# First stage of a two-layer diffusion step: loads and modulation products in another order, modulation ends and first norm scheduled ahead

## Chip, cores and metric

One NeuronCore of a Trainium2 chip runs the whole program. The metric is the device time of one launch in microseconds (us). Everything is float32; products with a split operand run as three float32r products (high x high, high x low, low x high).

## What is computed

Two transformer-like layers over 384 tokens (128 prompt tokens, 256 latent tokens). What matters here is the opening of each layer and the one thing that runs beside it:

```python
mod = (silu(cond) @ w_mod + b_mod)          # (1, 6*1024): sh1, sc1, g1, sh2, sc2, g2
h = rms_norm(x, norm1) * (1 + sc1) + sh1    # input of every mixer
proj = h @ w_in                             # 1024 x 6048; its Hyena columns come first in the kernel
kf = hyena_filters(L, w1, b1, w2, b2, w3, freq)   # an MLP with sines, window, L1 norm, DFT
```

`kf` depends on no token, so it can be computed beside anything that comes before the long convolution. `h` needs x, two of the six parts of `mod` (shift, part 0, and scale, part 1), and so 2 x 4 MB of `w_mod`.

## The kernel before, in words

Tokens stand in columns: `xa` is 128 x 8 x 384, eight chunks of 128 channels. One program text is written as Python generators ("lines"), each `yield` a step, and `weave` (line 1334) takes steps from side lines at a rate per step of a main line. The text gives each instruction its place (priority); a planner then fixes at compile time the order on every engine, from priorities and from its own idea of durations. At run time each engine works through its own list in order. `tc.high_priority(offset=n)` counts the instructions in it as if they stood n places earlier in the text; `urgent(line, n)` (line 1318) does so for every step of a line. Nothing else decides the order.

The parts of the first stage:

- `filters(0, ...)` (line 440) is the Hyena filter. Its first step loads the MLP's inputs; then come two sine layers (`reduce_sin`, line 423, with a chain of eight VectorE/ScalarE instructions each, and one product each, lines 460 and 464); then `half_inputs(0)` loads `w3` and the window for one half of the channels and `kdft`, the DFT table; then `half_inputs(1)` the other half. After that come four jobs: `prep` (line 483), three `taps` (line 498, products of line 503), three `sizes` (line 517) and `spectra` (line 531, products of lines 538, 546 and 558).
- `mod_load` (line 326) loads one 1 MB slice of `w_mod`. `mod_vec(l, v)` (line 332) makes part v: for each of four slices k, four products of line 338 into one PSUM bank; then a ScalarE copy, four transposes (line 302) into the same bank, two small VectorE sums, and for part 1 the scale `avs` (line 241 as `stt`). The bank line `md` has one bank (bank 7), so part 1 starts after part 0's sums are out.
- `squares` (line 314) squares and adds the eight chunks of x. `norm_h` (line 373) makes the reciprocal root on a diagonal, spreads it over 128 partitions by a product (line 388), and then, chunk by chunk: multiply (VectorE), scale and shift on ScalarE (line 396, one for each token stream), and the split into high and low parts (lines 403 and 231, then a subtraction).
- `hyena_start` (line 615) issues two loads of `w_in` (`load_w`, line 247), each split by ScalarE (line 231) and VectorE (line 235) in two halves. The main line `hyena_in` (line 634) then makes six outputs of 8 x 3 products each (lines 269 to 271). Its first product needs the first chunk of h and the first half of the first weight load.

The eight early `w_mod` slices lie in buffers that later have another use: two in the raw ring of the weight loads, four in the slab of the split weights, two in the slab of h. Only SP issues loads in this stage. The order of the text was: MLP inputs, `vecs`, `cT`; the two sine layers; `half_inputs(0)` and `kdft`; `w_mod` 0/0 and 0/1 (part/slice), identity; `half_inputs(1)`; `w_mod` 0/2 and 0/3, both halves of x, `w_mod` 1/0 to 1/3, silu. Then a `weave` of the two `mod_vec` with three filter steps and 1.2 squares for each of their steps (12 steps of `mod_vec`, so 36 of the filter's 49 steps stand in it). Then `hyena_start`, the whole norm, the rope tables and the second `vecs`, and the loop over layers, whose first `weave` takes two filter steps for each step of `hyena_in`.

Of the kernel before, what the change touches and what calls it, by code (L numbers as in the profile page):

```python
# [41 lines left out]
SLABS = (1408, *[3072] * 9)  # L42
N_EXTRA = 3584
R_RE = 0.25
R_F0 = 3
U_CH, U_MLA = 20, 20
U_AV = 2000
FILL = (3, 2, 3)
# [137 lines left out]
def kernel(  # L186
# [127 lines left out]
    def squares():  # L314
        for k in range(KD):
            add_sq(k, xa[:, k], k == 0)
            yield
# [8 lines left out]
    def mod_load(l, v, k, buf):  # L326
        raw = buf.ap(2, 1024)
        src = w_mod[l, k * 256:(k + 1) * 256, v * 1024:(v + 1) * 1024]
        sp.dma_start(out=raw, in_=src.rearrange("(k p) n -> p k n", p=128))
        return raw  # L330

    def mod_vec(l, v, ready=(), bufs=()):

        gv = ps_of("md", 512)
        for k in range(KD // 2):
            raw = ready[k] if k < len(ready) else mod_load(l, v, k, raw_ring.get())
            for j in range(4):
                pe.matmul(  # L338
                    gv[32 * j:32 * j + 32], cT[:, 2 * k + j // 2], raw[:, j // 2, (j % 2) * 512:(j % 2) * 512 + 512],
                    start=k == 0, stop=k == KD // 2 - 1, tile_position=(0, 32 * j),  # L340
                )
            if bufs:
                bufs.pop(0).free()
            yield
        ms = mod_s
        copy_a(ms.ap(), gv)
        yield
        pm = ps_of("md", 4, 128)
        for q in range(4):
            transpose(pm[:, q], ms.ap()[:, q * 128:(q + 1) * 128])  # L350
# [89 lines left out]
    def filters(l, R, spec, first=False):  # L440
# [8 lines left out]
        def half_inputs(hf):  # L449
            w3 = FA.alloc(4, 256)  # L450
            sp.dma_start(out=w3.ap(1024), in_=p_w3[l, hf])
            wb = FA.alloc(5, 256)
            sp.dma_start(out=wb.ap(1280), in_=p_win[l, hf])
            return wb, w3
# [14 lines left out]
        h.free()  # L469
        yield  # L470
        inputs = [half_inputs(0), None]
        kd = [FA.alloc(10, 128)] if first else [R.alloc(10, 128) for _ in range(2)]
        kt = [b.ap() for b in kd]
        kv = t_kdft.rearrange("p (a b) -> p a b", b=128)
        if first:
            sp.dma_start(out=kt[0], in_=kv)
        yield
        if first:
            inputs[1] = half_inputs(1)
            yield  # L480
        jobs = {}
# [847 lines left out]
    def finish(*lines):  # L1329
        for g in lines:  # L1330
            for _ in g:
                pass
# [11 lines left out]
    def chain(*lines):  # L1344
        for g in lines:
            yield from g
# [21 lines left out]
    next(fl)  # L1368
    sp.dma_start(out=vecs[0], in_=p_vec[0])
    sp.dma_start(out=cT, in_=p_c)  # L1370
    next(fl)
    next(fl)
    next(fl)
    ready = [mod_load(0, 0, k, early[k]) for k in range(2)]
    sp.dma_start(out=ident, in_=t_ident)
    next(fl)
    for k in (2, 3):
        ready.append(mod_load(0, 0, k, early[k]))
    for k in (0, 4):
        sp.dma_start(out=xa[:, k:k + 4], in_=p_x[:, k:k + 4])  # L1380
    for k in range(4):
        ready.append(mod_load(0, 1, k, early[4 + k]))
    act.activation(out=cT[:, :, 0:2], in_=cT[:, :, 0:2], func=AF.Silu)
    weave(chain(mod_vec(0, 0, ready[:4]), mod_vec(0, 1, ready[4:])), (fl, R_F0), (squares(), 1.2))
    for b in early_parts:
        b.free()
    parts = split_slab.whole(F32R).cut(1024)
# [2 lines left out]
    h_parts += [b.ap(KD, T) for b in h_slab.whole(F32R).cut(KD * T)]  # L1390
    hT = h_parts
    y, main = hyena_start(0, spec)
    finish(norm_h(0, 0))
    for i in range(2):
        rt = t_rope[i * 128:(i + 1) * 128]
        sp.dma_start(out=rope_a[:, i], in_=rt[:, 0:128].rearrange("p (a b) -> p a b", a=2))
        sp.dma_start(out=rope_b[:, i], in_=rt[:, 128:192].rearrange("p (a b) -> p a b", a=2))
    sp.dma_start(out=vecs[1], in_=p_vec[1])
    for l in range(NL):
        md = chain(*[mod_vec(l, v) for v in (2, 3, 4, 5)]) if l == 0 else chain(nxt.pop().steps, mod_vec(l, 4))  # L1400
        banks(**PS_HY0)
        weave(main, (md, R_MD), (fl, R_FL))
        finish(fl)
        hyena_open(y)
        oC = y.oT
        banks(**PS_HY1)
# [196 lines left out]
```

## Time and profile before

| | us |
|---|---|
| runs: median of 3 (lowest, highest) | 1504.46 (1504.19, 1507.05) |
| profiled execution, its own time | 1503.74 |
| span of the profiled execution | 1501.6 |
| TensorE busy, of the span | 1455.7 |
| VectorE busy | 1006.0 |
| ScalarE busy | 751.3 |
| mean rate of the loads over the span | 142 GB/s |

The time of an execution is its span and 2.1 us around it. In the rows below PE is TensorE (PEld its weight loads), DVE VectorE, ACT ScalarE, POOL GpSimd, SP the engine that issues loads; "L338" is line 338. A timeline row has the start, the time the (merged) instructions took, the engine, the line, the operation with what it writes and reads, the count, and in brackets how long the engine sat idle before it and what ended that. `base`, `split`, `h` and `s` are memory slabs: a load of `w_in` lands in `base` and is split into `split`, and `banks` is PSUM. A float32 product is recorded as two.

### The profile page before, as it was taken

What the parts mean: (1) busy time and instruction counts of PE and PEld (TensorE: products, weight loads), DVE (VectorE), ACT (ScalarE), POOL (GpSimd) and SP (SyncE); (2) the same over time, 40 slices, a digit from 0 to 9 for tenths busy, and PEclk for the clock granted to TensorE, in tenths of its full rate; (3) what the DMA queues carried; (4) which work ended last, traced back from release to release, by engine and by line L of the source; (5) the groups of instructions that cost most, each with busy time, mean ns of one, the idle gap of its engine ahead of it and who ended that gap; (6) DMA issues with size and microseconds to landing.
All of it is one profiled execution on the core that took longest, in us unless ns stands there. A gap on an engine that the chain in (4) does not pass through costs nothing.

```text
span 1501.6 us, 22071 instructions
## 1 busy us (share of the span) xinstructions
PE 1455.7 (97%) x8542; PEld 1337.6 (89%) x8542; DVE 1006.0 (67%) x1920; ACT 751.3 (50%) x1376; POOL 106.4 (7%) x133
## 2 busy tenths in 40 slices
PE   5799999999999999999998999999999999999997
PEld 2588789989889899999996988999888989999997
DVE  6768569547457896686766767884655767567674
ACT  4545356555544663463545444855555454344343
POOL 1223210000000001010000212100000000000000
PEclk9899999999999999999999999999999999999999
DMA  9444454433466543343276446332333523433431
GB/s 362 151 153 138 136 166 138 119 113 113 141 224 228 187 137 103 122 130 113 85 246 204 139 135 182 91 106 83 97 118 111 195 100 117 135 105 122 153 119 50
DMA packets 177496, 212.84 MB, mean 142 GB/s; under 512 B 24176, under 2 KB 160112, under 8 KB 177392
## 3 DMA queue, kind: packets, MB, share of 16 engines
q1 hardware_dynamic: 176528, 206.99, 42.7%
q0 software_dynamic: 864, 4.46, 1.0%
q8 instruction: 67, 1.10, 0.3%
q14 instruction: 37, 0.30, 0.1%
HBM read 209.29 MB, written 2.13 MB: 141 GB/s over the span
## 4 chain that ended last, share of the span: by engine, by line
PE 90%; DVE 4%; ACT 3%; DMA 2%; issue 1%; SPq 0%; DVEq 0%; ACTq 0%
PE banks L269 26%; PE banks L270 26%; PE banks L271 25%; PE banks L302 3%; PE banks L338 3%; PE banks L922 3%; DVE s L238 2%; PE banks L954 2%; DMA base<-in_w_in_dram 1%; DVE split L235 1%; PE banks L558 1%; ACT split L231 1%; ACT s L231 1%; PE banks L503 0%; DVE s L241 0%
## 5 line engine op out<-in xcount | busy, mean ns | idle before, releaser
L231 ACT ACTIVATE split<-base 128x1024 fp32r<-128x1024 f32 (+2 forms) x272 | 280.9, 1041 | 366.9 <-PE banks L270 258.5
L235 DVE TENSOR_TENSOR split<-base,split 128x1024 fp32r<-128x1024 f32 (+2 forms) x272 | 331.8, 1225 | 181.5 <-ACT split L231 179.4
L269 PE MATMUL banks<-h,split 128*128 128x384 f32 x1280 | 433.3, 342 | 5.0 <-DVE h L403 3.6
L270 PE MATMUL banks<-h,split 128*128 128x384 f32 x1280 | 435.2, 340 | 0.1
L271 PE MATMUL banks<-h,split 128*128 128x384 f32 x1280 | 434.2, 340 | 0.0
L269 PEld LDWEIGHTS banks<-h,split 128*128 128x128 f32 x1280 | 241.4, 189 | 20.7 <-issue 9.9
L270 PEld LDWEIGHTS banks<-h,split 128*128 128x128 f32 x1280 | 242.0, 189 | 4.5 <-issue 1.3
L271 PEld LDWEIGHTS banks<-h,split 128*128 128x128 f32 x1280 | 241.7, 189 | 2.2 <-issue 0.5
L270 PE MATMUL banks<-s,split 128*128 128x384 f32 x672 | 225.8, 337 | 0.0
L271 PE MATMUL banks<-s,split 128*128 128x384 f32 x672 | 225.4, 338 | 0.0
L269 PE MATMUL banks<-s,split 128*128 128x384 f32 x672 | 223.2, 339 | 1.0 <-ACT s L231 0.8
L241 DVE SCALAR_TENSOR_TENSOR s<-banks,base,s 128x127 f32<-128x127 f32 (+1 forms) x448 | 172.8, 411 | 11.9 <-ACT s L417 7.9
L231 ACT ACTIVATE s<-banks 128x384 f32<-128x384 f32 (+11 forms) x212 | 94.3, 471 | 99.1 <-PE banks L271 37.9
L231 ACT ACTIVATE s<-s 128x384 fp32r<-128x384 f32 (+3 forms) x142 | 79.0, 562 | 106.0 <-DVE s L238 57.2
L269 PEld LDWEIGHTS banks<-s,split 128*128 128x128 f32 x672 | 125.6, 188 | 4.4 <-ACT s L231 1.4
L271 PEld LDWEIGHTS banks<-s,split 128*128 128x128 f32 x672 | 126.1, 188 | 2.0 <-DVE base L241 0.8
L270 PEld LDWEIGHTS banks<-s,split 128*128 128x128 f32 x672 | 126.1, 188 | 1.4 <-issue 0.2
L238 DVE TENSOR_TENSOR s<-banks,s 128x512 f32<-128x512 f32 (+3 forms) x132 | 81.6, 645 | 37.7 <-PE banks L271 16.7
L241 DVE SCALAR_TENSOR_TENSOR base<-banks,base 128x128 f32<-128x128 f32 (+1 forms) x128 | 46.9, 413 | 73.8 <-PE banks L271 73.8
L238 DVE TENSOR_TENSOR s<-s 128x256 f32<-128x256 f32 (+4 forms) x122 | 69.0, 576 | 23.0 <-ACT s L1225 8.4
L417 ACT ACTIVATE s<-banks,base 128x384 f32<-128x384 f32 x112 | 73.2, 655 | 13.2 <-PE banks L271 13.2
L302 PE MATMUL banks<-base,s 128*128 128x128 f32 x442 | 75.2, 274 | 2.8 <-DVE s L241 1.7
(146 smaller groups left out, 1730.4 us busy)
## 6 DMA issues: line engine op xcount, KB each, us to landing
base<-in_w_in_dram SPq DMA_DIRECT2D x40, 1024.0 KB, 5.4
base<-in_ffn_up_dram SPq DMA_DIRECT2D x40, 1024.0 KB, 5.1
base<-in_w_mod_dram SPq DMA_DIRECT2D x28, 1024.0 KB, 5.3
s<-in_w_mod_dram SPq DMA_DIRECT2D x14, 1024.0 KB, 7.5
base<-in_ffn_down_dram SPq DMA_DIRECT2D x16, 896.0 KB, 4.6
base<-in_w_branch_dram SPq DMA_DIRECT2D x24, 512.0 KB, 3.5
base<-in_w_out_dram SPq DMA_DIRECT2D x8, 1024.0 KB, 5.1
base<-in_ffn_down_dram SPq DMA_DIRECT2D x8, 1024.0 KB, 5.0
```

The lines of the kernel that those rows point to most:

```text
L231: act.activation(out=out, in_=in_, func=AF.Copy, scale=scale)
L235: dve.tensor_tensor(out=lo, in0=src, in1=f(hi), op=ALU.subtract)
L238: dve.tensor_tensor(out=out, in0=a, in1=b, op=op)
L241: dve.scalar_tensor_tensor(out=out, in0=a, scalar=s, in1=b, op0=op0, op1=op1)
L269: pe.matmul(out, l[0], r[0], start=start, stop=False)
L270: pe.matmul(out, l[0], r[1], start=False, stop=False)
L271: pe.matmul(out, l[1], r[0], start=False, stop=stop)
L302: pe.transpose(out, in_, ident[:n, :n])
L338: pe.matmul(gv[32 * j:32 * j + 32], cT[:, 2 * k + j // 2], raw[:, j // 2, (j % 2) * 512:(j % 2) * 512 + 512], start=k == 0, stop=k == KD / ...
L417: act.activation(out=dst, in_=src, func=AF.Identity, scale=vec(l, w1), bias=vec(l, bias))
L922: pe.matmul(out, q_of(h)[:, i * 128:(i + 1) * 128], k, start=m == 0, stop=m == len(ks) - 1)
L954: last = pe.matmul(p[b:b + 64, u], v, pT, start=start, stop=stop, tile_position=(0, b)).ins
```

## The change

The filter's steps 4 and 5 are cut differently: the step that loads `half_inputs(0)` now ends there, and `kdft` and `half_inputs(1)` are steps 5 and 6. The loads stand in the text as: MLP inputs, `vecs`, `cT`, silu, `w_mod` 0/0 and 0/1; then after the first sine layer the products of these two slices; after the second the identity, `half_inputs(0)`, `w_mod` 0/2, `kdft`, `w_mod` 0/3, x, `w_mod` 1/0 and 1/1, `half_inputs(1)`, `w_mod` 1/2 and 1/3. The end of a modulation part is a function of its own, `mod_end`, without the step between copy and transposes, and for parts 0 and 1 of layer 0 it is placed 300 instructions ahead; the first norm is placed 150 ahead. `mod_vec` has five steps in place of six, two of them are taken before the `weave`, and the filter's rate in it is 3.5: eight main steps, 28 filter steps. The rope tables and the second `vecs` are loaded after the `weave` of `hyena_in`.

```diff
--- before.py
+++ after.py
@@ -42,7 +42,8 @@
 SLABS = (1408, *[3072] * 9)
 N_EXTRA = 3584
 R_RE = 0.25
-R_F0 = 3
+R_F0 = 3.5
+U_MD, U_N0 = 300, 150
 U_CH, U_MLA = 20, 20
 U_AV = 2000
 FILL = (3, 2, 3)
@@ -342,9 +343,13 @@
             if bufs:
                 bufs.pop(0).free()
             yield
+        with ExitStack() as order:
+            order.enter_context(tc.high_priority(offset=U_MD if (l, v) in ((0, 0), (0, 1)) else 0))
+            yield from mod_end(l, v, gv)
+
+    def mod_end(l, v, gv):
         ms = mod_s
         copy_a(ms.ap(), gv)
-        yield
         pm = ps_of("md", 4, 128)
         for q in range(4):
             transpose(pm[:, q], ms.ap()[:, q * 128:(q + 1) * 128])
@@ -469,13 +474,13 @@
         h.free()
         yield
         inputs = [half_inputs(0), None]
+        yield
         kd = [FA.alloc(10, 128)] if first else [R.alloc(10, 128) for _ in range(2)]
         kt = [b.ap() for b in kd]
         kv = t_kdft.rearrange("p (a b) -> p a b", b=128)
         if first:
             sp.dma_start(out=kt[0], in_=kv)
-        yield
-        if first:
+            yield
             inputs[1] = half_inputs(1)
             yield
         jobs = {}
@@ -1368,20 +1373,24 @@
     next(fl)
     sp.dma_start(out=vecs[0], in_=p_vec[0])
     sp.dma_start(out=cT, in_=p_c)
+    act.activation(out=cT[:, :, 0:2], in_=cT[:, :, 0:2], func=AF.Silu)
+    ready = [[mod_load(0, 0, k, early[k]) for k in range(2)], []]
+    md = chain(*[mod_vec(0, v, ready[v]) for v in range(2)])
     next(fl)
+    next(md)
+    next(md)
     next(fl)
-    next(fl)
-    ready = [mod_load(0, 0, k, early[k]) for k in range(2)]
     sp.dma_start(out=ident, in_=t_ident)
     next(fl)
-    for k in (2, 3):
-        ready.append(mod_load(0, 0, k, early[k]))
+    ready[0].append(mod_load(0, 0, 2, early[2]))
+    next(fl)
+    ready[0].append(mod_load(0, 0, 3, early[3]))
     for k in (0, 4):
         sp.dma_start(out=xa[:, k:k + 4], in_=p_x[:, k:k + 4])
-    for k in range(4):
-        ready.append(mod_load(0, 1, k, early[4 + k]))
-    act.activation(out=cT[:, :, 0:2], in_=cT[:, :, 0:2], func=AF.Silu)
-    weave(chain(mod_vec(0, 0, ready[:4]), mod_vec(0, 1, ready[4:])), (fl, R_F0), (squares(), 1.2))
+    ready[1] += [mod_load(0, 1, k, early[4 + k]) for k in (0, 1)]
+    next(fl)
+    ready[1] += [mod_load(0, 1, k, early[4 + k]) for k in (2, 3)]
+    weave(md, (fl, R_F0), (squares(), 1.2))
     for b in early_parts:
         b.free()
     parts = split_slab.whole(F32R).cut(1024)
@@ -1390,17 +1399,18 @@
     h_parts += [b.ap(KD, T) for b in h_slab.whole(F32R).cut(KD * T)]
     hT = h_parts
     y, main = hyena_start(0, spec)
-    finish(norm_h(0, 0))
-    for i in range(2):
-        rt = t_rope[i * 128:(i + 1) * 128]
-        sp.dma_start(out=rope_a[:, i], in_=rt[:, 0:128].rearrange("p (a b) -> p a b", a=2))
-        sp.dma_start(out=rope_b[:, i], in_=rt[:, 128:192].rearrange("p (a b) -> p a b", a=2))
-    sp.dma_start(out=vecs[1], in_=p_vec[1])
+    finish(urgent(norm_h(0, 0), U_N0))
     for l in range(NL):
         md = chain(*[mod_vec(l, v) for v in (2, 3, 4, 5)]) if l == 0 else chain(nxt.pop().steps, mod_vec(l, 4))
         banks(**PS_HY0)
         weave(main, (md, R_MD), (fl, R_FL))
         finish(fl)
+        if l == 0:
+            for i in range(2):
+                rt = t_rope[i * 128:(i + 1) * 128]
+                sp.dma_start(out=rope_a[:, i], in_=rt[:, 0:128].rearrange("p (a b) -> p a b", a=2))
+                sp.dma_start(out=rope_b[:, i], in_=rt[:, 128:192].rearrange("p (a b) -> p a b", a=2))
+            sp.dma_start(out=vecs[1], in_=p_vec[1])
         hyena_open(y)
         oC = y.oT
         banks(**PS_HY1)
```

## Rows read from the trace of the kernel before

**Rows 1.** Page, first part, whole span: engine, busy us, share, instructions.
```profile
PE 1455.7 (97%) x8542; PEld 1337.6 (89%) x8542; DVE 1006.0 (67%) x1920; ACT 751.3 (50%) x1376; POOL 106.4 (7%) x133
```

**Rows 2.** Windows, first stage: us, busy per engine, PEclk, DMA share, GB/s.
```profile
25.00:30.00 5.00, 4.91 (x32) 3.80 (x24) 4.17 (x8) 4.31 (x10) 2.42 (x3) 1.00 1.01 411
...
35.00:40.00 5.00, 4.09 (x19) 1.36 (x17) 3.47 (x8) 3.09 (x5) 1.06 (x2) 1.00 1.06 364
...
50.00:55.00 5.00, 3.91 (x20) 2.45 (x18) 5.00 (x9) 2.12 (x3) 1.82 (x1) 1.00 0.51 145
55.00:60.00 5.00, 0.00 (x0) 0.00 (x0) 5.00 (x9) 0.63 (x1) 1.58 (x1) 0.57 0.25 73
60.00:65.00 5.00, 4.80 (x12) 4.08 (x13) 4.11 (x13) 4.99 (x12) 1.44 (x2) 0.50 0.57 201
65.00:70.00 5.00, 5.00 (x26) 3.43 (x26) 3.50 (x9) 5.00 (x13) 0.00 (x0) 0.90 0.24 52
```

**Rows 3.** Timeline, TensorE: start us, us, engine, line, operation, count [idle before].
```profile
47.31 1.06 PE L338 MATMUL banks<-h,base 128*32 128x512 f32 x8
...
49.80 0.66 PE L302 MATMUL banks<-base 128*128 128x128 f32 x4 [0.37 <-ACT base L231]
...
60.20 1.22 PE L558 MATMUL banks<-s 128*128 128x256 f32 x2 [5.93 <-DVE s L540]
...
63.42 1.52 PE L269 MATMUL banks<-h,split 128*128 128x384 f32 x3
```

**Rows 4.** Timeline, VectorE, from the transposed sums to the last normed chunk.
```profile
53.01 0.17 DVE L238 TENSOR_TENSOR base<-banks,base 128x16 f32<-128x16 f32 x1
...
54.02 2.06 DVE L235 TENSOR_TENSOR split<-base,split 128x1024 fp32r<-128x1024 f32 x1
...
59.26 0.16 DVE L238 TENSOR_TENSOR base<-base,banks 128x16 f32<-128x16 f32 x1
...
60.06 0.17 DVE L241 SCALAR_TENSOR_TENSOR base<-base 128x16 f32<-128x16 f32 x1
...
72.33 1.02 DVE L235 TENSOR_TENSOR h<-s,h 128x384 fp32r<-128x384 f32 x2
```

**Rows 5.** Load issues: last w_mod slices, SP timeline, then us to landing.
```profile
L329 SPq DMA_DIRECT2D h<-in_w_mod_dram x2: 1440/1925/2410, 17.9 to 19.5; - x2
...
33.53 18.16 SPq L249 DMA_DIRECT2D base<-in_w_in_dram  x3
...
h<-in_w_mod_dram SPq DMA_DIRECT2D x1, 1024.0 KB, 20.7
...
base<-in_w_in_dram SPq DMA_DIRECT2D x1, 1024.0 KB, 10.8
```

**Rows 6.** Groups of TensorE products, 46 to 63.4 us: count, busy us, mean ns.
```profile
L558 PE MATMUL banks<-s,s 128*128 128x256 f32 x11 | 3.8, 472 | 0.0
L558 PE MATMUL banks<-s 128*128 128x256 f32 x4 | 2.3, 674 | 5.9 <-DVE s L540 5.9
L503 PE MATMUL banks<-s 128*128 128x512 f32 x6 | 2.3, 479 | 0.4 <-DVE s L238 0.4
L546 PE MATMUL banks<-s,base 128*128 128x512 f32 x2 | 1.1, 644 | 0.0
...
L538 PE MATMUL banks<-base,s 128*128 128x1 f32 x8 | 1.0, 249 | 0.0
```

**Rows 7.** Timeline, start of the filter work: VectorE, then TensorE.
```profile
7.60 0.43 DVE L238 TENSOR_TENSOR s<-s 128x256 f32<-128x256 f32 x1 [1.74 <-DMA s<-in_p_w_dram]
...
8.21 1.08 DVE L238 TENSOR_TENSOR s<-s 128x256 f32<-128x256 f32 x3
...
9.60 0.69 DVE L238 TENSOR_TENSOR s<-s,s 64x512 fp32r<-64x512 f32 x1
...
13.75 1.65 PE L464 MATMUL banks<-s 64*128 64x384 f32 x2 [8.60 <-ACT s L436]
...
16.46 0.15 PEld L338 LDWEIGHTS banks<-base 128*32 128x32 f32 x4 [0.93 <-DMA base<-in_w_mod_dram]
```

## Prediction

> **What bounds the kernel now.** The page comes first: TensorE is busy 97% of the span [rows 1], so a change pays only where TensorE is idle or slow. The windows tell where that is. From 65 us on TensorE is full; before, 55 to 60 us holds no product at all, and 60 to 65 us runs at a granted clock of 0.50, the 1.2 GHz level, after 0.57 in the stretch before [rows 2]. VectorE is the full engine there: 5.00 of 5.00 us in both windows from 50 to 60 us [rows 2].
>
> The timeline of TensorE shows what comes out late. The last products of modulation part 1 start at 47.31 us, their transposes at 49.80, and the first product of the main line at 63.42; between lies the idle stretch of 5.93 us that ends at 60.20 [rows 3]. The timeline of VectorE says why. The transposes end at 50.46 (49.80 + 0.66), but the two sums that read them run at 53.01 and 59.26 and the scale at 60.06 [rows 3, 4]: three instructions of 0.16 to 0.17 us, spread over 7 us in VectorE's list, among splits of weights (two in 2.06 us at 54.02) and filter work. No operand is missing; the order put them there. Norm and main line wait for the scale, which is out at 60.23.
>
> The last `w_mod` slice does not explain it: issued at 19.5 us, it lands 20.7 us later, at 40.2, but its products start 7.1 us after that [rows 3, 5]. The transfers are the floor under all this, as the load engines are fully busy (1.01) at 411 GB/s [rows 2].
>
> **The change, part by part.**
>
> *Modulation end ahead.* New start of the last products: about 40.4. The bytes before that slice are the same, and the order inside them does not move the last one. From there to the scale: product to end of the transposes took 3.15 us (47.31 to 50.46) [rows 3], in which ScalarE was also splitting a weight, so this is rather an upper price; the three small instructions add 0.50 [rows 4] if VectorE takes them at once, and about 0.2 for their handovers by my estimate. Scale out at 44.2 at the latest, 43.4 without ScalarE's delay; I take 43.8. That is 16.4 us earlier than 60.23.
>
> *Norm ahead.* The step from scale to first main product was 3.2 us (60.23 to 63.42) [rows 3, 4]; I keep it: first product at 47.0. The part of the norm that needs no modulation (root, spread, four of the chunk products, as the eight buffers of `temps` hold four pairs) lies before that, beside the loads. The weights must not be later: the first `w_in` load was issued at 33.53 and landed 10.8 us after, at 44.3 [rows 5]. Its split costs one ScalarE and one VectorE instruction, about 1.03 us each by VectorE's pair in 2.06 [rows 4], so it is ready at 46.4. It is the next thing in line, half a microsecond behind.
>
> *Work owed.* An earlier start is not all gain: the filter products that filled 46 to 63.4 us must still run, now beside a full TensorE. They are L558 3.8 and 2.3, L503 2.3, L546 1.1 and L538 1.0 us [rows 6]. The 2.3 ran at half clock (674 ns each against 472 in a mixed stretch [rows 6]), so I count it and the 3.8 as 3.6 together: 8.0 us owed. Bounds: 6.8, if some of it still fits before 47, and 10.5, all as recorded. The modulation products, transposes and the norm's own product also stood in that stretch; they go in front of 47, where TensorE waits anyway, and cost nothing. 16.4 - 8.0 = 8.4 us.
>
> *Clock.* The main line's first 2.6 us (63.4 to 66) ran at half clock, inside the windows of 0.50 and 0.90 [rows 2]. Without the idle stretch this gives 1.3 back: 9.7.
>
> *Filter starts earlier.* In the old order the first two `prep` instructions wait 1.74 us for `w3` and then, with their like, sit in the middle of the first sine layer: 0.43, 1.08, 0.69 and, at 10.90, 0.69 more, of which one is shown [rows 7]. The second layer's product at 13.75 had idled TensorE for 8.60 us [rows 7]. With `w3` loaded later these 4.6 us leave the chain; that is the upper bound. The products of slices 0/0 and 0/1 now stand ahead of that product on TensorE, and norm and modulation go ahead of filter work on VectorE and ScalarE for about 3 us before 47; the lower bound is -1. I take +1.5, less than half, since VectorE was the full engine: 11.2.
>
> *Pace of the norm.* From 63.42 to the end of the last chunk's split at 73.35 it took 9.9 us for eight chunks [rows 3, 4], seven steps of 1.4. A chunk frees three products (0.17 us each at full clock) for each of two open outputs, 1.04 us. What is left, 0.36 x 7 = 2.6, was filled by filter products before (5.00 of 5.00 from 65 [rows 2]); now the filter is behind norm and splits on VectorE. Between 0 and 2.6 I take 1.2: 10.0.
>
> *Rope tables and second `vecs` moved.* They leave the end of the load stream. Rows: the rate falls from 411 to 364 GB/s from 35 to 40 us with the load engines still fully busy [rows 2]; that costs (411 - 364) x 5 us = 0.24 MB, or 0.6 us, if nothing else slows it. The Trainium skill ("DMA: Bandwidth & Descriptors", Why small descriptors are slow) says that short descriptors from HBM move below full rate, for a fixed cost of each packet. By that reading the tables, in runs of 512 and 256 bytes, would be this loss, and the sum would be 10.6; the trace agrees with a slower stretch, but doesn't show whose packets. I keep 10.0. In their new place they stand on SP's queue between loads of the main line, where the load engines are a third to half busy (0.24 to 0.57 in 60 to 70 us [rows 2]), and the rope tables are wanted only in attention: nothing.
>
> *Others.* Silu moved ahead waits for the same small load and costs nothing. The filter of layer 1 takes its DFT buffers a step later; it has the whole feed-forward part beside it. All else in the planner's order may shift by itself: +-1.5 us by my guess, in the range only.
>
> **Sum.** 16.4 - 8.0 + 1.3 + 1.5 - 1.2 = 10.0 us. Own time of the profiled execution 1503.74, so 1493.7; the median of the runs is 0.7 above it, so **1494.5**. With all bounds on one side the gain is 5 or 14.5.
>
> **Rivals.**
>
> *The filter takes it back.* VectorE stays the full engine for what follows, since splits, norm and filter are the same work in less time. Then TensorE gains only what it stood idle (5.9) and the half clock (1.3), less the pace (2.6): 4.6, or 1499.9. For it: two windows with VectorE at 5.00. Against: 3.50 from 65 to 70 us [rows 2].
>
> *Half clock at the new start.* The skill ("TensorE: Matmul & The Clock Gate", HAM oscillation — how this bites in real kernels) says that products in short groups with waits on loads between them let the array's clock fall, again and again. Here TensorE would have little but filter products from 41.5 (last slice) to 47. Rows: an idle stretch of 5.93 us was followed by the window of 0.50 [rows 2, 3]. If a stretch like it comes before 47, the first 5.8 us of products (60.2 to 66) again run at half rate: 2.9 less, gain 7.1, 1497.4. Against: filter products are at hand, and from 25 to 30 us, with waits on loads, the granted clock was 1.00 [rows 2]. By that rule the trace agrees for the one long stretch only.
>
> *The lists wait in order (slower).* An instruction placed 300 ahead also blocks its engine if its operand is later than planned. If the planner lets the last slice land early, ScalarE's copy and VectorE's sums stand in front of the filter and everything waits. The deciding point: the wait must cost the 10 us gained and 3 more, so the plan must be 13 us early at this one place; that gives 1507.5. For it: nothing in VectorE's list could pass. Against: the longest wait of a `w_mod` product on its slice was 0.93 us [rows 7], so plan and chip agree to about a microsecond.
>
> *It doesn't do what it says.* The offsets rank instructions only among those ready in the plan; if the sums stay behind the splits and the weight split replaces them as last, the gain is 0 to 2: 1503.
>
> **Chances.** Forecast 0.58, filter takes it back 0.15, half clock 0.13, no effect 0.07, slower 0.05, a larger gain (all upper bounds) 0.02. A measurement of this kernel tells 0.2%, 3.0 us, from no change, so faster means under 1501.5: the first three and the larger gain nearly whole, 0.87; same 0.08; slower 0.05. The range goes from 1489.5 (the upper bounds) to 1501, which takes in the two smaller gains.
>
> **What would show it.** Right: the scale's instruction (L241 on `base`) at 43 to 45 us, right behind the transposes; the first L269 at 46 to 48; no window before it without products and none at 0.50 after it; last chunk split near 57; the L558 groups spread further into the main line. Wrong in a step: L338's last group well after 41 (transfers or order), the scale out but L269 waiting for `split` (weights are the next wait), windows from 47 to 60 with gaps in TensorE and VectorE at 5.00 (the filter takes it back). Wrong altogether: first L269 after 58, or a gap elsewhere that was not there.

## Result and the profile after

The change makes the kernel slower. Median 1514.61 us of 4 runs (1510.88 to 1514.96) against 1504.87 of 4 (1504.19 to 1507.05): ratio 1.0056, 95% interval 1.0041 to 1.0071 (taken over all runs, not the quotient of the two medians, which is 1.0065). Forecast were 1494.5 us and a range of 1489.5 to 1501.0, so the sign was wrong. The profiled execution is the quickest of the four, 1510.88 us with a span of 1509.1: 7.1 us above the profiled execution of before, so the profile can account for 7.1 of the 9.7 us between the medians; the other three stand at 1514.5 to 1515.0, with a mean granted clock of 0.989 for 0.992.

The page's first part answers to [rows 1]: same instructions, TensorE 7.9 us busier.

```profile
PE 1463.6 (97%) x8542; PEld 1338.0 (89%) x8542; DVE 1005.7 (67%) x1920; ACT 752.1 (50%) x1376; POOL 110.0 (7%) x133
```

The windows of the first stage, after, columns as in [rows 2]:

```profile
35.00:40.00 5.00, 4.76 (x17) 2.19 (x17) 3.41 (x12) 3.72 (x8) 0.70 (x1) 0.67 1.05 376
...
45.00:50.00 5.00, 2.74 (x22) 1.47 (x20) 4.16 (x12) 3.03 (x5) 3.87 (x3) 1.00 0.04 15
50.00:55.00 5.00, 2.08 (x2) 0.50 (x2) 2.60 (x4) 5.00 (x13) 0.73 (x1) 0.70 0.35 75
55.00:60.00 5.00, 3.06 (x7) 2.28 (x8) 4.93 (x10) 5.00 (x9) 0.00 (x0) 0.50 0.39 136
60.00:65.00 5.00, 5.00 (x21) 4.34 (x21) 4.90 (x11) 4.49 (x11) 0.00 (x0) 0.78 0.50 158
```

The hole in TensorE has moved from 55 to 60 us to 50 to 55, and the stretch at half clock with it. The full engine there is now ScalarE (5.00 of 5.00 in both windows from 50 to 60; VectorE has 4.93 in the second), where it was VectorE [rows 2].

The timeline of TensorE, after, answers to [rows 3]; its first two rows are the second sine product and the filter's first products:

```profile
11.40 1.65 PE L469 MATMUL banks<-s 64*128 64x384 f32 x2
...
21.12 3.74 PE L508 MATMUL banks<-s 128*128 128x512 f32 x8 [0.85 <-ACT s L232]
...
45.20 1.06 PE L339 MATMUL banks<-h,base 128*32 128x512 f32 x8
...
47.11 0.63 PE L303 MATMUL banks<-base 128*128 128x128 f32 x4
52.46 2.08 PE L551 MATMUL banks<-s,base 128*128 128x512 f32 x2 [4.71 <-ACT s L232]
56.85 1.79 PE L270 MATMUL banks<-h,split 128*128 128x384 f32 x3 [2.32 <-DVE h L408]
```

The timeline of VectorE, after, from the transposed sums to the first normed chunk [rows 4]:

```profile
47.85 0.18 DVE L239 TENSOR_TENSOR base<-banks,base 128x16 f32<-128x16 f32 x1
...
48.46 0.13 DVE L239 TENSOR_TENSOR base<-base,banks 128x16 f32<-128x16 f32 x1
48.63 0.44 DVE L242 SCALAR_TENSOR_TENSOR base<-base 128x16 f32<-128x16 f32 x1
49.80 2.36 DVE L236 TENSOR_TENSOR split<-base,split 128x1024 fp32r<-128x1024 f32 x2 [0.74 <-ACT split L232]
...
54.99 0.36 DVE L408 CAST h<-s 128x384 fp32r<-128x384 f32 x1 [1.61 <-ACT s L401]
```

The timeline of ScalarE in the same stretch, after:

```profile
48.73 1.99 ACT L232 ACTIVATE split<-base 128x1024 fp32r<-128x1024 f32 x2
50.62 0.97 ACT L232 ACTIVATE s<-base,s 128x128 f32<-128x128 f32 x3
51.50 0.61 ACT L232 ACTIVATE s<-s 1x512 f32<-1x512 f32 x1
52.02 0.38 ACT L232 ACTIVATE s<-base,s 128x128 f32<-128x128 f32 x1
52.31 0.61 ACT L526 ACTIVATE s<-s 128x512 f32<-128x512 f32 x1
52.83 3.60 ACT L401 ACTIVATE s<-s,base 128x128 f32<-128x128 f32 x8
```

The sums and the scale do follow the transposes at once: the scale is out at 49.07 (48.63 + 0.44), 11.2 us earlier than before. But the norm's own ScalarE work starts only at 52.83, behind two splits and filter copies, so the first main product comes at 56.85: 6.6 us earlier than before, not 16.4.

Even these 6.6 us are gone soon. Counting the products of the main line's three lines (L269 to L271 of before) from the first on, by the timeline:

| start of the n-th product, us | 1st | 72nd | 144th | 500th | 1000th | 1500th |
|---|---|---|---|---|---|---|
| before | 63.4 | 81.8 | 104.6 | 175.9 | 290.9 | 413.4 |
| after | 56.9 | 81.3 | 102.2 | 183.4 | 296.4 | 425.9 |
| after, minus before | -6.5 | -0.5 | -2.4 | +7.5 | +5.5 | +12.5 |

Six outputs of 24 products are 144. The filter's last product (L558) starts at 98.1 before and at 114.9 after. The second norm of layer 0 (L388; L393 after) shows more than the whole loss of the profiled execution, 9.4 us, and what follows gives back 2 of them. TensorE's timeline of before at that place:

```profile
488.80 0.91 PE L388 MATMUL banks<-s,base 128*128 128x384 f32 x2
```

and of after:

```profile
498.23 0.91 PE L393 MATMUL banks<-s,base 128*128 128x384 f32 x2
```

### The profile page after: what moved, and what is told of

It is laid out like the page before. It is cut to its first block, busy times and chain, and to the rows that moved or that the text cites. A ratio compares the mean times of both kernels' runs of the same rounds, so it can differ in the third digit from the quotient of the medians.

```text
span 1509.1 us, 22075 instructions
## 1 busy us (share of the span) xinstructions
PE 1463.6 (97%) x8542; PEld 1338.0 (89%) x8542; DVE 1005.7 (67%) x1920; ACT 752.1 (50%) x1376; POOL 110.0 (7%) x133
## 4 chain that ended last, share of the span: by engine, by line
PE 92%; DMA 2%; ACT 2%; DVE 2%; SPq 1%; issue 0%; POOL 0%; DVEq 0%; ACTq 0%
PE banks L270 27%; PE banks L271 26%; PE banks L272 26%; PE banks L303 3%; PE banks L339 3%; PE banks L927 3%; PE banks L959 2%; PE banks L563 1%; DMA base<-in_p_x_dram 1%; DMA base<-in_w_mod_dram 1%; SPq L1411 1%; ACT s L232 1%; DVE s L239 1%; PE banks L508 0%; DMA base<-in_p_vec_dram 0%
## 5 line engine op out<-in xcount | busy, mean ns | idle before, releaser
L271 PE MATMUL banks<-h,split 128*128 128x384 f32 x1280 | 433.5, 339 | 0.2
L271 PEld LDWEIGHTS banks<-h,split 128*128 128x128 f32 x1280 | 241.1, 188 | 4.8 <-issue 1.9
L271 PE MATMUL banks<-s,split 128*128 128x384 f32 x672 | 225.7, 337 | 0.0
L232 ACT ACTIVATE s<-banks 128x384 f32<-128x384 f32 (+10 forms) x212 | 94.4, 472 | 115.1 <-PE banks L272 41.9
L271 PEld LDWEIGHTS banks<-s,split 128*128 128x128 f32 x672 | 126.1, 188 | 1.5 <-issue 0.2
L236 DVE TENSOR_TENSOR s<-s,s 128x512 fp32r<-128x512 f32 (+2 forms) x102 | 64.4, 634 | 23.9 <-ACT s L232 19.9
```

What stands on the lines that cost most here:

```text
L232: act.activation(out=out, in_=in_, func=AF.Copy, scale=scale)
L236: dve.tensor_tensor(out=lo, in0=src, in1=f(hi), op=ALU.subtract)
L271: pe.matmul(out, l[0], r[1], start=False, stop=False)
```

## Where TensorE's time goes

To see what fills it I took TensorE's timeline up to this norm product, gave each row the time from its start to the next row's start less the idle time in the next row's brackets, and summed by line. "Modulation" is L338 of before, "filter" L503, L538, L546 and L558, "transposes" L302 (in the others the same lines of text, a few numbers on), "main" L269 to L271, "rest" all others. "Idle" is the time in the brackets. With the start (3.6 to 3.8 us) a column gives the norm's instant. Each column is one execution; that of steps28 (experiment 7) took 1515.74 us, 3.0 above that kernel's median, so it shows more than the usual loss.

| us | before | after | order_only | steps28 | before_grouped | after_grouped |
|---|---|---|---|---|---|---|
| modulation | 35.9 | 41.9 | 37.7 | 42.3 | 31.0 | 31.3 |
| filter | 32.7 | 35.0 | 34.6 | 34.3 | 32.9 | 34.7 |
| transposes | 23.3 | 24.2 | 26.9 | 24.9 | 22.6 | 24.7 |
| main | 336.5 | 335.9 | 339.7 | 339.8 | 335.5 | 335.6 |
| rest | 34.5 | 35.4 | 36.2 | 35.8 | 35.5 | 34.0 |
| idle | 22.2 | 22.2 | 26.5 | 22.5 | 22.6 | 21.9 |
| norm at | 488.8 | 498.2 | 505.3 | 503.3 | 483.9 | 486.0 |

From before to after idle time is the same; 6.0 of the 9.4 us are modulation products and 2.3 filter products, the same number of them in both kernels. Why modulation products should last longer is seen in the timeline, after, in layer 0's main line:

```profile
223.92 0.34 PE L272 MATMUL banks<-h,split 128*128 128x384 f32 x1
224.19 1.04 PE L339 MATMUL banks<-base 128*32 128x512 f32 x2
225.16 0.45 PE L270 MATMUL banks<-h,split 128*128 128x384 f32 x1
225.54 1.05 PE L339 MATMUL banks<-base 128*32 128x512 f32 x2
226.51 0.33 PE L303 MATMUL banks<-base,s 128*128 128x128 f32 x1
226.77 1.04 PE L339 MATMUL banks<-base 128*32 128x512 f32 x2
227.75 0.44 PE L271 MATMUL banks<-h,split 128*128 128x384 f32 x1
```

A float32 product is recorded as two, so each "x2" is one of the four products of a slice (four strips of 32 columns). From its start to the next product's it takes 0.97 to 0.98 us, alone. Four together take no more: in after_grouped (below) all four of a slice stand in one row,

```profile
183.88 1.07 PE L344 MATMUL banks<-base 128*32 128x512 f32 x8
184.87 0.39 PE L270 MATMUL banks<-s,s 128*128 128x256 f32 x1
```

0.99 us. So a slice whose four products are split up in TensorE's list costs a "turn" of 1 us for each piece. From 60 to 420 us I count 22 pieces for 15 slices before, and 27 for 16 after; over the whole span, 57 turns for 48 slices before and 61 after. The groups by line and shape of these 360 us (count, busy us, mean ns), before:

```profile
L338 PE MATMUL banks<-base 128*32 128x512 f32 x120 | 23.3, 605 | 0.0
```

after:

```profile
L339 PE MATMUL banks<-base 128*32 128x512 f32 x128 | 28.5, 605 | 0.0
```

and after_grouped:

```profile
L344 PE MATMUL banks<-base 128*32 128x512 f32 x128 | 17.0, 604 | 0.0
```

One record lasts 604 to 605 ns in all three; only the company differs. The Trainium skill ("TensorEngine Tiling (Array Packing)", Key Properties of the tiling modes) says that a change of the tiling mode, unlike one of the tile, drains the engine; the 1 us of a lone product among full-width ones agrees with that, though no run here separates a drain from the time of the product itself.

## Experiments

Each gives the median, then in brackets the ratio to the kernel before on the same chip and its 95% interval. "Scale" is the start of its instruction, and a "bound" group is one whose four products must follow one another in TensorE's list. Theories in the expectations: A, the new load order costs; B, the offsets cost; C, later stages cost because their lists are planned anew; D, late filter inputs and half clock in the first stage; E, the early products and the 28 filter steps in place of 36; F, broken groups of four; the others are stated where they come.

**1. The change without its offsets**: `U_MD, U_N0 = 0, -1`.

> The changed kernel with both offsets taken away (0 for the modulation ends, none for the first norm); loads, products and steps in the new order. Theory A, the load order costs: the filter's inputs land late (first half 14 us for 7.6, second half 33 for 18), so the filter's products slide behind 60 us; this kernel then keeps the whole loss, 1510 to 1516 us, and its first main product comes at 60 us or later. Theory B, the offsets cost (norm and modulation push filter work off ScalarE and VectorE): without them the loss is gone, 1500 to 1506. Theory C, the later stages' lists are planned anew and cost by themselves: the first 140 us are level with before within 2 us and the loss arises between 140 and 500 us.

1517.41 us (1.0083, 1.0065 to 1.0101). Without the offsets the scale comes at 52.96 and the first main product at 56.95: the offsets move the scale by 4 us and the main line by 0.1. B falls, as the loss stays. Against A, the main line starts early and not at 60 us or later. The 144th main product starts at 100.9, ahead of before (104.6), and the 500th at 183.7, behind it (175.9): the loss arises where C puts it. But it is another loss than the change's: 22 pieces only, but TensorE waited 3.48 us on ScalarE at 227.36, and its windows show the granted clock below full:

```profile
220.00:230.00 10.00, 6.52 (x38) 5.17 (x37) 6.34 (x11) 4.99 (x10) 5.98 (x7) 0.84 0.73 242
230.00:240.00 10.00, 10.00 (x53) 10.00 (x52) 4.27 (x6) 3.62 (x8) 0.00 (x0) 0.81 0.07 18
...
330.00:340.00 10.00, 8.13 (x43) 7.04 (x41) 4.41 (x12) 4.43 (x9) 0.00 (x0) 0.83 0.33 106
```

**2. Only the offsets on the kernel before** (with the merged end of a modulation part, rate 3.6, so 36 filter steps; old loads).

> The kernel before with only the offsets (300 for the two modulation ends, with copy and transposes in one step; 150 for the first norm); filter rate 3.6, so that 36 filter steps stand in the weave as before; loads as before. Theory A: scale out near 50 us for 60.2, first main product near 55, total 1496 to 1501. Theory B: filter work is pushed back and the total is 1508 to 1514. Theory C: the first 140 us gain 2 to 5 us, and the total differs from that by up to 5 us either way.

1499.28 us (0.9964, 0.9951 to 0.9977): faster, so B falls here too. Yet not by the way forecast: the scale is at 61.99 and the first main product at 67.97, both later than before. It is not the first stage that gains: at the second norm the profiled execution stands at 489.17 us, before at 488.80. That execution (1501.92) is 2.6 us above the median, and where the quicker ones gain is not shown.

**3. The same, only the modulation offset** (`U_N0 = -1`).

> As the one with the offsets alone, but without the 150 for the norm. Theory A: the scale is out as early, the norm follows filter work on ScalarE, so the first main product comes 2 to 4 us later than with both offsets; total 1498 to 1504. Theory B: most of the loss was the norm's, so this is within 2 us of before. Theory C: any total between 1499 and 1510, with no relation to the first main product.

1505.5 us (1.0006, 0.9996 to 1.0016). Scale at 59.53, first main product at 62.44, no gain.

**4. The change once more**, beside the first three.

> The changed kernel once more, as it is: its executions stood at 1510.9 (granted clock 0.992 over the span) and three times near 1514.7 (0.989). If the two levels come from TensorE's clock in the first stage, the slower execution has one more stretch at 0.50 before 70 us, and the lists and landings are the same; a profile of it would show some 3 to 4 us more of half-rate products there. If they come from the loads, a landing is late instead.

1511.7 us (1.0049, 1.0029 to 1.0068). Its profiled execution, at 1511.57 us, does have one more window at half clock:

```profile
45.00:50.00 5.00, 3.87 (x20) 2.42 (x12) 2.84 (x10) 3.82 (x7) 2.78 (x3) 0.50 0.01 3
```

Yet its second norm comes at 497.13 us, 1.1 earlier than in the first profile. So this stretch costs nothing that is left there, and the 3 to 4 us between the levels stay open.

**5. Only the loads of the change on the kernel before** (its products, its 36 steps and six-step modulation parts stay).

> The kernel before with only the loads in the new order; products, steps (36 filter steps in the weave, six steps per modulation part) and places as before. Theory D, the load order alone delays the filter (its first half lands at 14 for 7.6 us, its second at 33 for 18), TensorE idles longer and runs at half clock: 3 to 5 us of products behind before at 60 us, first main product at 60 or later, total 1509 to 1517. Theory E, the early products and the 28 steps do it: this kernel is within 3 us of before.

1504.39 us (1.0002, 0.9993 to 1.0012): nothing. A falls.

**6. The change with the old order of the loads.**

> The changed kernel with the loads back in the old order (the text still takes two products ahead of the weave, 28 filter steps in it, both offsets). Theory D: the filter starts as before, so at 60 us the products are level with before or ahead, and the total is 1495 to 1502. Theory E: it stays near the changed kernel, 1509 to 1515.

1511.65 us (1.0052, 1.0032 to 1.0071): as the change. A falls from this side too.

**7. The kernel before with the merged step and 28 filter steps in the first interleave**, no offsets.

```diff
-R_F0 = 3
+R_F0 = 2.8
+U_MD, U_N0 = 0, -1
...
-        yield
```

(The cut line is that between copy and transposes, as in the change; what moves the code into `mod_end` is left out.)

> The kernel before with copy and transposes of a modulation end in one step and 28 filter steps in the weave in place of 36; no offsets, loads as before. If fewer filter steps ahead of norm and weight splits are what brings the scale forward, it is out at 50 to 53 us (before 60.1, offsets alone 62.0), the first main product comes at 54 to 57, and the total is 1496 to 1502. If the load order is what brings it forward, the scale stays near 60 us and the total at 1502 to 1506.

1512.77 us (1.0058, 1.0037 to 1.0079): the loss of the change without its loads, its early products and its offsets. The scale is at 49.77 and TensorE's timeline has the first main product 9 us earlier than before:

```profile
54.36 1.01 PE L270 MATMUL banks<-h,split 128*128 128x384 f32 x2 [1.88 <-DVE h L408]
```

Both times in the first stage were as expected for few filter steps, but the total was 10.8 us above the range expected with them. Experiment 12 is the same kernel with 36 steps (`R_F0 = 3.6`), and takes 1503.81 us. So what brings the main line forward is that eight filter steps stand behind it in the text, and this same thing loses the time, 9 us. The 500th main product is at 181.6, 5.7 us later than before.

**8. The change with the clock kept up**: eight more products with zero weights per early slice, which add nothing to the sums (from its diff):

```diff
+            for n in range(8 if zeros else 0):
...
+                    gv[32 * j:32 * j + 32], zeros[0], raw[:, j // 2, (j % 2) * 512:(j % 2) * 512 + 512],
```

> The changed kernel with eight more products behind each of the eight w_mod slices' four, with a zero stationary operand (they add zeros, about 2 us per slice at full clock), so that TensorE is busy between the landings. If the half clock between 9 and 60 us is a main part of the loss, the filter's first products (eight in 3.7 us in the changed kernel) take about 2.1 as before, no window before 50 us shows 0.50 to 0.78, and the total is level with the changed kernel or 1 to 4 us better in spite of up to 16 us more products. If the clock matters little, the added products only stand in the way: 3 to 10 us slower.

1515.43 us (1.0074, 1.0059 to 1.009). Its windows:

```profile
45.00:50.00 5.00, 5.00 (x39) 2.31 (x36) 4.94 (x6) 2.49 (x4) 3.85 (x2) 1.00 0.01 1
50.00:55.00 5.00, 0.97 (x9) 0.73 (x8) 5.00 (x10) 4.82 (x9) 1.79 (x2) 1.00 0.37 91
```

The clock holds up to 55 us and the taps run in 2.11 us for 3.74. The total is 0.8 us above the change's median, and 3.7 above experiment 4's, between what D and its rival gave. The scale is late (55.44) behind the added work, the first main product comes at 62.20, and from 55 to 65 us the clock is at 0.51 and 0.50 all the same. So this experiment doesn't decide on D; the next one does.

**9. The change with 36 filter steps**: `R_F0 = 4.5` for 3.5.

> The kernel after with one number changed: 36 filter steps go into the first stage's interleave, as before, where the change took 28 (R_F0 4.5 for 3.5); loads, early products and both offsets as in the change. Theory E (the eight filter steps put off cost the time, since their work is repaid by 100 us and the lists of layer 0 are then planned over other work): the scale comes late again (some 55 to 60 us) and yet the time falls to 1499 to 1504 us, as with before plus offsets (1499.3). Theory H (the early products and the load order cost by themselves): 1510 to 1515 us still. Theory G (neither decides; every rearrangement of the first stage lets the planner draw other lists for 140 to 350 us, better or worse by up to 10 us): anywhere from 1497 to 1515, and nothing between the scale's instant and the end agrees.

1505.18 us (1.0005, 0.9996 to 1.0014): 9.4 us back (6.5 by the median of experiment 4), 1.2 us above E's range and far from H's. E stands: scale at 53.62, first main product at 67.73, and the loss gone. D falls: the first taps are as slow as in the change (3.78 us), the windows from 35 to 45 us show 0.68 and 0.64 and those from 60 to 70 us 0.57 and 0.75, and the loss is gone in spite of it.

**10. The change with the groups of four bound.**

```diff
+            last = None
             for j in range(4):
-                pe.matmul(
...
+                with ExitStack() as order:
+                    if last is not None:
+                        order.enter_context(tc.high_priority(offset=U_AV))
+                        order.enter_context(tc.issue_after(last))
+                    last = pe.matmul(
...
+                    ).ins
```

> The kernel after, with the four products of each quarter slice of a modulation vector bound to follow one another in TensorE's list (they write four different strips of 32 columns). In the list of the change 192 such products stand in pieces that need 61 turns of up to four, where 48 would do; before it is 57. In the trace of the change a turn takes 0.98 to 1.06 us whether it holds one product or four. Theory F (broken groups carry a good part of the loss): 13 turns fewer give back up to 13 us, and 4 of them what the change lost against before; the time falls to 1500 to 1506. Theory G or E alone: a piece is not a turn lost, other work goes beside it; 1509 to 1514 as the change.

1499.89 us (0.9971, 0.9958 to 0.9984): 14.7 us less than the change's median and 11.8 less than experiment 4's, just below what F allowed. 16 pieces for 16 slices from 60 to 420 us in place of 27, and of the 12.2 us won by the second norm 10.6 are modulation products (table above). The first stage is as in the change (first main product 57.0).

**11. Experiment 2 with bound groups.**

> The kernel before with the merged modulation step and both offsets, 36 filter steps and the old loads (1499.3 us without more), and with the four products of each quarter slice bound to follow one another. 56 turns become 48. Theory F: 8 turns of some 1 us give 1491 to 1495 us. If pieces cost nothing of their own: 1497 to 1502.

1495.97 us (0.9938, 0.9922 to 0.9955): 3.3 us less than without, where F gave 4 to 8; it lies between F and its rival.

**12. Only the merged step on the kernel before** (36 filter steps).

> The kernel before with the modulation vector's last two steps merged into one and nothing else: 36 filter steps, old loads, no offsets. It tells what the merged step is worth, which was made in every kernel of this change beside what it names. The work done by TensorE in the kernels with it catches up some 2 to 5 us near 800 to 850 us, the border of layer 0 and 1, where the copy and the turning follow one another without another job's step between. Theory: that gain stays and nothing else moves, 1500 to 1503 us. If it is only the planner's draw (theory G): 1504 to 1512.

1503.81 us (0.9995, 0.9986 to 1.0005). The merged step is worth nothing by itself, a little less than I expected. Experiment 2 is this kernel with the offsets, and 0.31% faster; two more pairs that differ in both offsets alone agree, the change against experiment 1 (0.27%) and experiment 11 against 16 (0.26%). As experiment 3 has the modulation offset without a gain, the norm's seems to carry it; how is not shown.

**13. The kernel before with bound groups, nothing else.**

> The kernel before with the four products of each quarter slice of a modulation vector bound to follow one another, and nothing else (57 turns become 48; the merged step and the offsets are not in it). If the broken groups are the cost (theory F): 9 turns of 0.98 us less what the end of the kernel takes back, 1495 to 1500 us. If binding helps only beside the change's order: 1502 to 1506.

1494.83 us (0.9944, 0.9927 to 0.996). 8.5 us less than the kernel before (1503.29 beside it), as expected of 9 turns. Summed as in the table, modulation products behind 60 us take 8.5 us less in the profiled execution: 6.8 up to the second norm for 7 turns, 1.7 later for 2. That the total is the same is partly luck: those before 60 us take 1.9 us more, and other products in layer 1 some 4 us less.

**14. The change with both mends, 36 steps and bound groups.**

> The kernel after with both mends: 36 filter steps for 28 (1505.2 us alone) and the bound groups of four (1499.9 us alone). Theory E through F (the 28 steps cost time because they break more groups and leave half-rate products, and bound groups are cured of that): little over the bound groups alone, 1496 to 1501 us. Theory E by itself (28 steps cost some 9 us whatever the groups do): 1489 to 1493 us.

1497.58 us (0.9958, 0.9943 to 0.9973). The two mends do not add up: 14.7 + 9.4 would have given 1490.5. That is E through F, as forecast; against experiment 10 the 36 steps gain 0.13%, within the intervals.

**15. Experiment 7 with bound groups.**

> The kernel before with the merged step and 28 filter steps in the first stage's interleave (1512.8 us without more; 62 turns), with the groups of four bound (48 turns). Theory E through F: 14 turns fewer give most of the loss back, 1497 to 1502 us. Theory E by itself (the eight steps put off cost the time at another place): 1505 us or more.

1496.7 us (0.9956, 0.9942 to 0.9971), 16.1 us less than steps28. With the groups bound the number of filter steps makes no difference clear of the intervals: 1496.7 with 28, 1498.49 with 36 (experiment 16, which differs in this alone). So the loss needs both, the 28 steps and groups that may be broken. That it comes from the broken groups themselves is shown only for the part that the turns account for, as binding draws the lists anew as well.

**16. The merged step and bound groups on the kernel before** (36 steps, no offsets).

> The kernel before with bound groups of four (1494.8 us) and the merged last step of a modulation vector, 36 filter steps, no offsets, old loads. In the profiles with bound groups, layer 1's stretch from its first norm's spreading product to its second's took 399.2 us without the merged step (799.1 to 1198.3) and 403.4, 403.5 and 403.9 in the three kernels with it. Theory S (the merged step costs some 4 us in layer 1 once the groups are bound): 1497.5 to 1500.5 us and a stretch near 403.5. Rival (it is the rest of the change, or the draw of the lists): 1493 to 1496.

1498.49 us (0.9964, 0.9951 to 0.9977). Layer 1 between its two spreading products, TensorE's timeline of before_grouped:

```profile
799.08 0.91 PE L393 MATMUL banks<-s,base 128*128 128x384 f32 x2 [0.78 <-DVE s L390]
...
1198.30 0.91 PE L393 MATMUL banks<-s,base 128*128 128x384 f32 x2 [0.66 <-DVE s L390]
```

and of merge_grouped:

```profile
799.67 0.91 PE L398 MATMUL banks<-s,base 128*128 128x384 f32 x2 [0.77 <-DVE s L395]
...
1203.15 0.91 PE L398 MATMUL banks<-s,base 128*128 128x384 f32 x2 [0.66 <-DVE s L395]
```

399.2 against 403.5 us: theory S holds here, the merged step costs 4 us in layer 1 once the groups are bound. Without binding it is the other way: 404.0 us in before, 402.0 in experiment 12. So the price hangs on the list, not on the step alone.

**17 and 18. The step put back for layer 1**, in the change with bound groups and in experiment 11.

```diff
+        if l:
+            copy_a(mod_s.ap(), gv)
+            yield
```

> The change with bound groups (1499.9 us), and the step between copy and transposes put back for the modulation vectors of layer 1 (layer 0 keeps the merged one). Theory S: 1494.5 to 1497 us, and the stretch of layer 1 is near 399 us again. Rival: 1498 to 1501.5.

> The old loads and 36 filter steps with both offsets and bound groups (1496.0 us), and the step put back for layer 1. Theory S: 1490.5 to 1493.5 us, under every kernel so far. Rival: 1494.5 to 1497.5.

1497.58 us (0.9959, 0.9944 to 0.9974) and 1494.23 us (0.9932, 0.9915 to 0.9948): 2.3 and 1.7 us won, between what theory S and its rival gave, and within the intervals of the ratios. Layer 1's stretch is 401.0 and 401.5 us, half of the 4 us. How much the merged step costs in the change itself stays open.

The best kernels are prio_grouped_step and before_grouped, 0.7 and 0.6% under the kernel before; their intervals overlap, and the second needs only the diff of experiment 10.

## Why the prediction was wrong

By its steps:

- *Transfers.* Right. The last slice was issued at 22.4 and landed 17.2 us later, at 39.6 (in before 40.2), by the loads of after:

```profile
L330 SPq DMA_DIRECT2D h<-in_w_mod_dram x2: 378/640/902, 19.9 to 22.4; - x2
...
h<-in_w_mod_dram SPq DMA_DIRECT2D x1, 1024.0 KB, 17.2
```

- *Modulation end ahead.* Half wrong. I set the last products at the landing, 40.4; they came at 45.20, 5.6 us after the landing, with filter products (L508, waiting for VectorE until 43.94) ahead of them in TensorE's list. From there to the scale it took 3.9 us, as forecast (3.4). That the offsets did this is mostly wrong: on the old order they brought neither scale nor main line forward (experiment 2), and in the change they move the scale by 4 of its 11.2 us and the main line by 0.1 (experiment 1). "It doesn't do what it says" held for the main line; the 28 steps brought it forward (experiment 7).
- *Norm ahead.* Wrong: 7.8 us from scale to first product, not 3.2. I looked at VectorE alone, and the next full engine was ScalarE, with two splits and filter copies ahead of the norm (rows above). I also took the row at 54.02 [rows 4] for two splits; it is one (x1), and others take 1.2 us, so the weight's readiness was 0.1 us too early.
- *Work owed.* Wrong in size. The rival "the filter takes it back" is what happened, and more: it left the idle time as a gain, and of the 6.6 us 0.5 were left at the 72nd main product, 2.4 at the 144th and none at the 500th. By the second norm the idle time was 22.2 us in both kernels.
- *Clock.* Wrong in sign, by the rival "half clock at the new start": 0.70, 0.50 and 0.78 from 50 to 65 us after an idle stretch of 4.71 us, and 0.67 from 35 to 40. The Trainium skill's rule quoted in the prediction ("TensorE: Matmul & The Clock Gate", HAM oscillation — how this bites in real kernels) speaks of waits on loads; here the clock fell as well after a wait on ScalarE.
- *Filter starts earlier.* Wrong. The second sine product came 2.35 us earlier (11.40 for 13.75 [rows 7]), but the first taps at 21.12, where before has them at 20.31. They ran at about half the pace, though both windows of 20 to 25 us show a granted clock of 1.00: 3.74 us for eight records, 2.14 before. That is 1.6 of the filter's 2.3 us in the table. TensorE's timeline of before:

```profile
20.31 2.14 PE L503 MATMUL banks<-s 128*128 128x512 f32 x8 [1.67 <-ACT s L231]
```

- *Pace of the norm.* Mis-sized by little. From the first main product to the end of the last chunk's split (66.00) it took 9.2 us, 9.9 before, with filter products in between as before; nothing of the 1.2 us came.
- *Rope tables.* Wrong. The text moved them behind the main line's `weave`; in SP's list they only went from ahead of the first `w_in` load (from 22.04 us in before) to behind it, as SP's timeline of after shows. My weighing of short descriptors was about a move that did not take place as I described it.

```profile
24.39 1.31 SPq L250 DMA_DIRECT2D base<-in_w_in_dram  x1
26.21 9.38 SPq L1411 DMA_DIRECT2D base<-in_t_rope_dram  x1
```

- *Others.* This is the step that failed. I put "all else in the planner's order" at +-1.5 us, by guess, and my rival on the slower side was a wait in the first stage. What came was no wait: from 60 to 420 us the new list breaks the modulation products into 27 pieces for 16 slices. Against before's 22 for 15, plus one for its sixteenth, these are 4 pieces more, 3.9 us. The other 2.1 of modulation's 6.0 us lie before 60 us, where four of the eight slices took 1.93 us or a little more for 1.06. They are not put down to the change: before_grouped, with the order of before, has 11.5 us there, where after has 11.7 and before 9.6. The filter's 2.3 lie in the first stage. The rows for this were there to be read: L338 beside other products, 23.3 us for 15 slices, 1.55 us each where 1 would do. My bounds were summed wrongly, too: by the terms as written the gain lies between 3.2 and 15.9 us, not 5 and 14.5. But no bound on the terms that I had reaches a loss.

What is shown: the eight filter steps carry the loss (undone in 9; 7 against 12, which differ in them alone), and with bound groups they carry none (10 against 14, 15 against 16). Theory C holds in that form: the time goes in layer 0's later work, which the edit doesn't touch. What is not shown: why the planner breaks more groups with 28 steps than with 36. Nor are pieces all of it: in the change they are 3.9 of the 9.4 us. order_only loses more with 22 pieces, with a wait and a lower clock; and of the 5.4 us that the profile of experiment 9 wins by the second norm (492.84), modulation products are 1.4 (24 pieces for 27). With the groups bound, change and before still differ by 0.27% (0.9971 against 0.9944), of the size of the intervals; the merged step may account for part of it.

## What to carry to other kernels

When a planner makes the lists, an edit in one stage can cost in another that it does not touch: follow one instant (a norm, the n-th product) through the whole span in both profiles, and find where the difference arises. Four products on strips of the array took the time of one here only where they stood next to each other in the list; count the pieces, and bind them. Before counting on an earlier start, look which engine is full next, and where the work that stood in the gap will go.

## What was not expected of the hardware

A product of 128x32 weights and 512 float32 columns among full-width products took 0.97 to 1.00 us of TensorE, whether one, two, three or four strips ran together. After idle stretches of 3.48 and 4.71 us windows show granted clocks of 0.81 (order_only, a mean over 10 us, part of it at the 1.2 GHz level) and 0.50 (after, that level throughout), in the middle of layer 0 as in the first stage.
